# Sums for the means of two LayerNorms as one-column matmuls on TensorE, their sums of squares on GpSimd

## The chip, the cores and the metric

The kernel runs on one core of one Trainium2 chip. The metric is device time in microseconds (us) of one execution. Engines carry the profile's names: PE (TensorE matmuls), PEld (TensorE weight loads), DVE (VectorE), ACT (ScalarE), POOL (GpSimd) and SP (SyncE, which issues the loads).

## The reference

One step of a four-layer backbone on 640 tokens (512 sample tokens and 128 prompt tokens) of 1024 features. Layer i has its own token mixer and then a gated ConvFFN. Every sub-layer first normalises its input and modulates it, and its result is added to the stream, which is normalised again:

```python
# Each sub-layer: h = LN(x)*(1+scale)+shift (adaLN from SiLU(cond)),
# x <- LayerNorm(ALPHA*x + gate*f(h)) (DeepNorm post-norm).
def _layer_norm(x, g=None, b=None):
    xf = x.astype(F32)
    mu = jnp.mean(xf, axis=-1, keepdims=True)
    var = jnp.mean(jnp.square(xf - mu), axis=-1, keepdims=True)
    y = (xf - mu) * lax.rsqrt(var + LN_EPS)
    ...

def _pool_mix(h, w_grp, scale):            # the mixer of layer 2
    ...
    p = (mean - hg.astype(F32)).astype(h.dtype)     # mean over a window of tokens, less h
    y = jnp.einsum('btgc,gcd->btgd', p, w_grp).reshape(B, T, D)
    return y * scale
```

So two LNs stand between any two sub-layers: the post LN of the one that ends and the pre LN of the one that begins, which here is called the inner LN.

## The kernel before, in words

Everything is held feature-major: the stream `x` is 8 ktiles of 128 features (partitions) by 640 tokens. Tokens are worked on in two halves. In most places half 0 is the first 256 tokens and half 1 the last 384; in front of the pooling, which reads neighbouring tokens, half 2 is the first 384 and half 3 the last 256. While one half goes through its two LNs, PE works on the other half or on the next sub-layer.

An LN sums over features, that is over the 8 ktiles and over the 128 partitions. `sums_new` makes two accumulators of a half, `sums_add` is called for each ktile as it is written: ACT squares it (L328 for the first ktile, L332 for the others), POOL adds the ktile to the sum of values (L333), and DVE or POOL adds the square to the sum of squares (`sums_end`, L339), one ktile late. `ln_stats` then sums both over the partitions with one-column float32 matmuls against a column `onesD` (L352: two sums times two or three tiles of 128 tokens, into a `st` bank of PSUM); a float32 matmul leaves two records in the trace. The small row of mean, square of the mean, variance and the power -1/2 follows on DVE, ACT, DVE and POOL (L356 to L360), and PE transposes mean and 1/std back over all partitions into `bc` banks (L372). `centre` subtracts the mean (L383), `ln1` multiplies by 1/std (L395), scales and shifts into `x` (L396), and calls `sums_add` for the inner LN; `ln2` does the inner LN's own multiplication (L404) and modulation (L414), whose result is `h`.

A boundary (layer, 0 or 1) is the pair of LNs behind a sub-layer: (1, 1) lies behind the FFN of layer 1 and in front of the pooling (halves 2 and 3), (2, 0) behind the pooling and in front of the FFN of layer 2 (halves 0 and 1). Around the pooling the program goes through four stages, each named here by a letter:

- A: the down projection of layer 1's FFN for half 3 (`project`, triples of matmuls L175 to L177) covers the LNs of half 2.
- B: the pooling of half 0 (`hw` for three token tiles L1072, then `mix(0)`, L1082 and L1089, whose products `evac` adds to `x` on DVE, L436) covers the LNs of half 3, and the post LN of half 0 follows.
- C: `hw` for the last two token tiles and `mix(1)` cover the inner LN of half 0.
- D: the first up-projections of layer 2's FFN in plain float32 for half 0 (`up_mm32`, L487, 64 matmuls) cover the two LNs of half 1. The triples L175 to L177 begin again behind them.

Order: each engine runs its instructions in the program's order, and where generators of two pieces of work are stepped against each other (`LN_A`, `LN_P`, `LN_B` say at which matmul which step of an LN is issued) the order comes from that and from the framework's own scheduling pass; the final order of each engine is fixed before the run. PSUM pools: `mm` 4 banks (products), `bc` 3, `st` 1. A name such as `mm_15657` in an order is one use of a buffer of pool `mm`.

Of the kernel before, what the change touches and what calls it, by code (L numbers as in the profile page):

```python
# [12 lines left out]
AF = mybir.ActivationFunctionType  # L13
# [4 lines left out]
NK = 8  # L18
TS = 512
TP = 128  # L20
T = TS + TP
# [12 lines left out]
# half 0 runs ahead of half 1, and 2 of 3 (in front of the pooling, which reads neighbours)  # L34
HALVES = ((0, 256), (256, 640), (0, 384), (384, 640))
HW = 384
# (start, stop, group) with group 0 = sample, 1 = prompt
SEGS = (((0, 256, 0),), ((256, 512, 0), (512, 640, 1)), ((0, 384, 0),), ((384, 512, 0), (512, 640, 1)))
# ktiles of the FFN between its down-projections
FFN_CHUNKS = ((0, 7), (7, 14), (14, 22))  # L40
SKEW = {None: 7, 2: 6, 3: 6, 1: 6, 0: 6}
# units of a projection's weights that half B finds from half A
KEEP = {None: 4, (0, 0): 3, (1, 1): 5, (3, 1): 5, (1, 0): 3, (3, 0): 5}
# layer 0's modulation, blocks of 512 features, in plain float32
MOD32 = (2, 0)
# SKEW ktiles of the FFN run half A ahead of half B, 2 SKEW units of weights: the last SPLIT of them in split parts
# (SPLIT_AHEAD units ahead of their use), of which half B finds the last KEPT; h is split SPLIT_H units from the end
SPLIT = {None: 6, 3: 11, 2: 4, 1: 7}
SPLIT_POOL = {None: False, 0: 1}
SPLIT_AHEAD = {None: 2, 0: 0}  # L50
SPLIT_H = {None: 12, 2: 11, 1: 14, 3: 5, 0: 14}
KEPT = 2
# steps of the next layer's modulation behind each product of an FFN
BG = {None: 1, 0: 0.95}
# heads of half A in split parts; units of weights ahead of them
A_SPLIT = 4
A_AHEAD = 1
# items of the attention between the scores and the transposes
LAG = 3
# tiles of tokens of half A per block of 512 features of v; units of weights ahead  # L60
VPRE = ((0, 1), (0, 1), (0,), ())
V_AHEAD = 5
# columns (tokens) that the window sums of a tile of 128 tokens reach; which band matrix of a group that is
BAND_RANGE = ((0, 136), (120, 264), (248, 392), (376, 512), (512, 640))
BAND_KIND = (0, 1, 1, 2, 3)
# tiles of the LN; ktiles that are centred ahead (of the two LNs of a half, and of the last)
# [3 lines left out]
# where the steps of an LN are issued (20: sums, broadcasts, 8 ktiles, and again for the next sub-layer's LN):  # L70
# LN_A half A's, in products (8 each) of half B; LN_B half B's (position, steps), in matmuls of half A of the next
# sub-layer; LN_P the same in the pooling
LN_A = {None: (8, 16, 16, 16, 16, 24, 24, 24, 32, 32, 40, 48, 48, 48, 48, 48, 56, 56, 56, 56), (0, 1): (4, 15, 20, 20, 26, 30, 30, 30, 33, 39, 45, 49, 49, 52, 53, 54, 61, 61, 62, 62), (2, 1): (6, 11, 16, 17, 21, 26, 26, 27, 33, 34, 48, 52, 57, 63, 63, 63, 63, 72, 76, 81), (0, 0): (0, 15, 15, 19, 22, 24, 26, 32, 37, 37, 48, 48, 58, 58, 59, 59, 60, 61, 70, 80), (1, 0): (5, 15, 17, 17, 17, 19, 21, 29, 29, 29, 44, 47, 51, 53, 53, 53, 58, 62, 73, 78), (1, 1): (10, 15, 15, 20, 20, 26, 30, 30, 33, 33, 47, 48, 60, 61, 61, 61, 61, 61, 61, 64), (3, 0): (9, 14, 17, 17, 20, 22, 22, 23, 26, 30, 43, 49, 49, 53, 53, 57, 57, 57, 60, 60), (3, 1): (8, 23, 23, 24, 24, 26, 30, 30, 30, 40, 41, 45, 55, 58, 60, 61, 67, 68, 68, 68)}
LN_B = {None: ((8, 1), (16, 9), (56, 1), (64, 9)), (0, 0): ((0, 1), (12, 9), (51, 1), (65, 9)), (2, 0): ((7, 1), (8, 9), (42, 1), (63, 9)), (1, 0): ((12, 1), (16, 9), (52, 1), (53, 9)), (0, 1): ((2, 1), (15, 9), (58, 1), (63, 9)), (2, 1): ((10, 9), (15, 1), (48, 1), (60, 9)), (3, 0): ((8, 1), (23, 9), (58, 9), (65, 1))}
LN_P = ((4, 1), (16, 1), (22, 4), (23, 3), (24, 1), (38, 2), (44, 2), (45, 1), (51, 1), (52, 3), (54, 1))

# columns of the packed per-partition vectors
# [33 lines left out]
class Kern:  # L111
# [45 lines left out]
    def unit(self, src, shape, e=None):  # L157
        """A piece of weights, split exactly into two float32r parts."""
        nc = self.nc
        r = self.raw(shape)  # L160
        self.load(r, src)
        hl = self.hlp.tile([128, 2] + list(shape[1:]), F32R, tag="hl", name=self.nm("hl"))
        nc.scalar.copy(hl[:, 0], r)  # L163
        (e or nc.vector).tensor_sub(hl[:, 1], r, hl[:, 0])  # L164
        return hl

    def split(self, dst, src, e=None):
        """dst [:, 0] + [:, 1] = src exactly."""
        self.nc.scalar.copy(dst[:, 0], src)  # L169
        (e or self.nc.vector).tensor_sub(dst[:, 1], src, dst[:, 0])  # L170

    def mm3(self, out, lhs, rhs, start, stop):
        """out += lhs^T rhs with (hi, lo) pairs of operands."""
# [8 lines left out]
    def table(self, f, x):  # L182
        """Has the tables of an activation function loaded ahead of its use, once x is there."""
        self.nc.scalar.activation(self.small("tab", [128, 1]), x.bitcast(F32), f)

    def consts(self):
# [27 lines left out]
        # modulation [part, chunk, ktile, group]  # L214
        self.mod = [cp.tile([128, 6, NK, 2], F32, name=f"mod{i}") for i in range(DEPTH)]

    def cond_rows(self):
        """silu(cond) along the free dimension, on every partition."""
# [10 lines left out]
    def mod_post(self, L, ft, n, ps, lo=None):  # L229
        """Feature tiles ft .. ft + n (of one chunk) of the modulation of layer L, from its sums [128, n, 2]."""  # L230
# [12 lines left out]
    def mod_mv(self, fb):  # L243
        """512 features of layer 0's modulation: w_mod streams through the tensor engine. Yields after each unit."""
        nc = self.nc
        ps = self.st([4, 512])
        for i in range(4):
            if fb in MOD32:
                # while the loads set the pace: plain float32, nothing to split
# [23 lines left out]
    def mod_dve(self, L, f0, f1):  # L273
        """Feature tiles f0 .. f1 as dot products on the vector engine. Yields after each product."""
# [15 lines left out]
    def bg(self, n):  # L290
        """n steps (on average) of the background work."""
# [18 lines left out]
    def sums_new(self, half):  # L310
        """Sums of z and z^2 over the ktiles, per partition, of a half."""
        w = HALVES[half][1] - HALVES[half][0]
        S = types.SimpleNamespace(first=None, last=None, pool=True, nt=w // 128, n=0)
        if w <= 256:
# [6 lines left out]
    def sums_add(self, S, z, t=None, scale=None, bias=None, pool=True):  # L321
        """S1 += z, S2 += z^2 on a ktile of a half, z = scale t + bias if t is given; the last square waits
        for sums_end."""
        nc = self.nc
        src, kw = (z, {}) if t is None else (t, dict(scale=scale, bias=bias))
        n, S.n = S.n, S.n + 1
        if n == 0:
# [5 lines left out]
        nc.gpsimd.tensor_add(S.s[0], z, S.s[0] if n > 1 else S.first)  # L333
        self.sums_end(S)
        S.last = sq

# [5 lines left out]
    def ln_stats(self, S, half, eps, together):  # L342
        """Mean and 1/std of the tokens of a half, broadcast over partitions, in PSUM. Yields once between the
        sums and the broadcasts, then the two."""
# [4 lines left out]
        st = self.st([128, 2, 3])  # L349
        for q in range(2):  # L350
            for t in range(S.nt):
# [4 lines left out]
        v.tensor_copy(cv[:, 0, n], st[:, 0, n])  # L356
        nc.scalar.activation(w[:, n], st[:, 0, n], AF.Square)
# [18 lines left out]
    def centre(self, MU, half, ahead):  # L376
        """The ktiles of x of a half less their mean, some ahead of their use."""
# [10 lines left out]
    def ln1(self, t, R, L, which, half, k, S=None):  # L388
        """x <- LN(z) g + b on a ktile of a half."""
# [10 lines left out]
    def ln2(self, t, R, L, ch, half, k, box):  # L400
        """h = LN(x)(1 + scale) + shift on a ktile of a half."""
# [18 lines left out]
    def late_steps(self, box):  # L420
        """(hi, lo) of half A of h."""
# [8 lines left out]
    def evac(self, ps, L, ch, m, half, gate=None):  # L430
        """z += gate' * product, in place in x."""
# [8 lines left out]
    def project(self, gs, units, L, ch, after, fill=None, halves=(0, 1)):  # L440
        """z += gate' W^T g; half A runs ahead so that its LN hides behind half B.

        gs: list of (hi, lo) tiles; units(m) -> weights as a function of the ktile."""
# [38 lines left out]
    def up_mm32(self, h32, w):  # L482
        """Half A of a product in plain float32."""
# [45 lines left out]
    def ffn_pre(self, L, box):  # L529
        """Half A of the first ktiles, while half B of h is not there yet: in plain float32, and the last of  # L530
        them in split parts, whose weights half B then uses first."""
# [28 lines left out]
    def ffn(self, L, box, side, after):  # L560
# [7 lines left out]
        def skew():  # L568
            """Half B of the first ktiles."""
# [63 lines left out]
    def boundary(self, L, which, box, pre=None):  # L633
        """after-callback: post LN of sub-layer (L, which) and the h of the next sub-layer."""
# [765 lines left out]
```

## Time and profile before

| | |
|---|---|
| median of 3 runs | 2803.09 us (2801.15 to 2807.25) |
| span of the profiled execution | 2805.7 us |
| PE busy | 2749.6 us (98%) |
| DVE busy | 1973.0 us (70%) |
| ACT busy | 1240.0 us (44%) |
| POOL busy | 407.5 us (15%) |
| mean granted TensorE clock | 0.987 of 2.4 GHz |

The profiled execution lies 0.1% above the median; its span, from the first to the last instruction, is the time of it that the profile gives. Busy time counts the engine's records; several records of PE overlap, so what a matmul costs PE is read from the distance of starts, not from the length of a record. A granted clock of 1.0 is 2.4 GHz and of 0.5 is 1.2 GHz.

### The profile page before, as it was taken

What the parts mean: (1) busy time and instruction counts of PE and PEld (TensorE: products, weight loads), DVE (VectorE), ACT (ScalarE), POOL (GpSimd) and SP (SyncE); (2) the same over time, 40 slices, a digit from 0 to 9 for tenths busy, and PEclk for the clock granted to TensorE, in tenths of its full rate; (3) what the DMA queues carried; (4) which work ended last, traced back from release to release, by engine and by line L of the source; (5) the groups of instructions that cost most, each with busy time, mean ns of one, the idle gap of its engine ahead of it and who ended that gap; (6) DMA issues with size and microseconds to landing.
All of it is one profiled execution on the core that took longest, in us unless ns stands there. A gap on an engine that the chain in (4) does not pass through costs nothing.

```text
span 2805.7 us, 46039 instructions
## 1 busy us (share of the span) xinstructions
PE 2749.6 (98%) x17826; PEld 2636.0 (94%) x17826; DVE 1973.0 (70%) x4263; ACT 1240.0 (44%) x2286; POOL 407.5 (15%) x417
## 2 busy tenths in 40 slices
PE   7999999999999999999999999999999999999998
PEld 4799999999989999999978999999799999999998
DVE  6879977857697887777587878775756558534344
ACT  5656232336496752323367423234532248423233
POOL 1250000024303300000442000005100042000003
PEclk9999999999999999999989999999999999999999
DMA  7735644432402445455104554542422224322221
GB/s 241 259 109 163 198 154 149 156 121 80 134 22 83 136 153 158 149 157 153 56 35 150 151 165 151 158 136 80 161 65 91 68 62 152 97 82 68 83 75 54
DMA packets 99932, 344.70 MB, mean 123 GB/s; under 512 B 11392, under 2 KB 14080, under 8 KB 99584
## 3 DMA queue, kind: packets, MB, share of 16 engines
q1 hardware_dynamic: 99712, 341.74, 38.7%
q8 instruction: 141, 2.31, 0.3%
q14 instruction: 79, 0.65, 0.1%
HBM read 336.19 MB, written 2.88 MB: 121 GB/s over the span
## 4 chain that ended last, share of the span: by engine, by line
PE 88%; DVE 5%; issue 2%; ACT 2%; DMA 2%; POOL 1%; POOLq 0%; ACTq 0%; SPq 0%; DVEq 0%
PE mm L175 26%; PE mm L176 26%; PE mm L177 26%; PE mm L487 2%; PE st L352 1%; PE mm L1157 1%; DVE hl L164 1%; DVE tmp L339 1%; DMA raw<-in_wmod 1%; PE mm L1247 1%; PE bc L372 1%; DVE lnt L383 1%; DVE act L170 0%; PE mm L1072 0%; DMA raw<-in_wup 0%
## 5 line engine op out<-in xcount | busy, mean ns | idle before, releaser
L177 PE MATMUL mm<-act,hl 128*128 128x384 f32 (+2 forms) x4928 | 1528.5, 310 | 3.2 <-DVE hl L164 3.2
L175 PE MATMUL mm<-act,hl 128*128 128x384 f32 (+2 forms) x4928 | 1531.5, 311 | 0.0
L176 PE MATMUL mm<-act,hl 128*128 128x384 f32 (+2 forms) x4928 | 1528.6, 310 | 1.2 <-POOL act L418 1.2
L177 PEld LDWEIGHTS mm<-act,hl 128*128 128x128 f32 x4928 | 935.1, 190 | 5.0 <-DVE hl L164 4.4
L176 PEld LDWEIGHTS mm<-act,hl 128*128 128x128 f32 x4928 | 935.9, 190 | 3.7 <-POOL act L418 1.8
L175 PEld LDWEIGHTS mm<-act,hl 128*128 128x128 f32 x4928 | 935.2, 190 | 3.2 <-ACT hl L163 0.6
L163 ACT CAST hl<-raw 128x1024 fp32r<-128x1024 f32 (+1 forms) x433 | 444.1, 1030 | 625.9 <-PE mm L177 560.1
L164 DVE TENSOR_TENSOR hl<-raw,hl 128x1024 fp32r<-128x1024 f32 (+1 forms) x428 | 526.0, 1231 | 67.4 <-ACT hl L163 65.1
L283 DVE SCALAR_TENSOR_TENSOR bc<-raw,cbc 128x512 f32<-128x512 f32 x608 | 406.2, 719 | 130.3 <-DMA raw<-in_wmod 130.0
L436 DVE SCALAR_TENSOR_TENSOR x<-mm,mod,x 128x256 f32<-128x256 f32 (+2 forms) x408 | 166.0, 434 | 200.4 <-PE mm L177 199.8
L514 DVE SCALAR_TENSOR_TENSOR tmp<-ap,vecs,tmp 128x512 f32<-128x512 f32 x352 | 170.5, 547 | 147.6 <-ACT tmp L512 147.4
L333 POOL TENSOR_TENSOR tmp<-x,tmp 128x256 f32<-128x256 f32 (+1 forms) x180 | 178.0, 993 | 153.2 <-DVE x L436 109.0
L527 POOL MEMSET ap<- 128x1 f32 x24 | 2.1, 99 | 1188.4 <-DVE tmp L514 735.3
L502 ACT COPY ap<-mm 128x256 f32<-128x256 f32 x88 | 33.0, 375 | 265.2 <-PE mm L177 265.2
L333 POOL TENSOR_TENSOR tmp<-x 128x256 f32<-128x256 f32 (+1 forms) x30 | 30.7, 1024 | 733.3 <-DVE x L436 694.5
L383 DVE TENSOR_TENSOR lnt<-x,bc 128x256 f32<-128x256 f32 (+1 forms) x240 | 109.6, 479 | 14.9 <-PE bc L372 14.4
L332 ACT ACTIVATE lnt<-x 128x256 f32<-128x256 f32 (+1 forms) x112 | 51.2, 467 | 133.3 <-DVE x L436 130.9
L516 ACT ACTIVATE tmp<-tmp 128x640 f32<-128x640 f32 x88 | 65.2, 740 | 100.4 <-DVE tmp L514 100.4
L169 ACT CAST act<-tmp 128x640 fp32r<-128x640 f32 x117 | 84.9, 726 | 52.1 <-DVE tmp L519 31.8
L512 ACT ACTIVATE tmp<-ap,vecs 128x512 f32<-128x512 f32 (+1 forms) x176 | 106.4, 658 | 0.0
L339 DVE TENSOR_TENSOR tmp<-tmp,lnt 128x384 f32<-128x384 f32 (+1 forms) x126 | 93.7, 745 | 14.1 <-ACT lnt L332 12.6
L487 PE MATMUL mm<-h,raw 128*128 128x256 f32 x416 | 101.2, 399 | 1.8 <-DVE lnt L404 1.8
(209 smaller groups left out, 2684.1 us busy)
## 6 DMA issues: line engine op xcount, KB each, us to landing
raw<-in_wup SPq DMA_DIRECT2D x216, 512.0 KB, 3.5
raw<-in_wmod SPq DMA_DIRECT2D x184, 512.0 KB, 3.5
raw<-in_wdn SPq DMA_DIRECT2D x64, 448.0 KB, 3.4
raw<-in_wdn SPq DMA_DIRECT2D x46, 512.0 KB, 3.6
raw<-in_wgv SPq DMA_DIRECT2D x24, 512.0 KB, 4.1
raw<-in_wgo SPq DMA_DIRECT2D x19, 512.0 KB, 3.9
raw<-in_wqk SPq DMA_DIRECT2D x18, 512.0 KB, 3.5
raw<-in_wgu SPq DMA_DIRECT2D x16, 512.0 KB, 3.5
```

Source lines behind the costliest of these rows:

```text
L163: nc.scalar.copy(hl[:, 0], r)
L164: (e or nc.vector).tensor_sub(hl[:, 1], r, hl[:, 0])
L175: t.matmul(out, lhs[0], rhs[0], start=start, stop=False)
L176: t.matmul(out, lhs[0], rhs[1], start=False, stop=False)
L177: t.matmul(out, lhs[1], rhs[0], start=False, stop=stop)
L283: nc.vector.scalar_tensor_tensor(out=self.bc(), in0=r[:, sl], scalar=1.0, in1=self.cbc[:, g, sl], op0=ALU.mult, op1=ALU.mult, accum_out=ac ...
L333: nc.gpsimd.tensor_add(S.s[0], z, S.s[0] if n > 1 else S.first)
L339: (self.nc.gpsimd if S.pool else self.nc.vector).tensor_add(S.s[1], S.s[1], S.last)
L383: self.nc.vector.tensor_sub(t, self.x[:, k, a:b], MU)
L436: nc.vector.scalar_tensor_tensor(out=self.x[:, m, s0:s1], in0=ps[:, s0 - a:s1 - a], scalar=sc, in1=self.x[:, m, s0:s1], op0=ALU.mult, op1= ...
L487: self.nc.tensor.matmul(ps, w[:, k, :], h32[:, k, :], start=k == 0, stop=k == NK - 1)
L514: nc.vector.scalar_tensor_tensor(out=c[:, sl], in0=ap[:, o + i:o + i + n], scalar=cw(i), in1=c[:, sl], op0=ALU.mult, op1=ALU.add)
```

## The change

At the boundaries listed in a new table `PE_MEAN`, which are (1, 1) and (2, 0), the inner LN gets its sums another way. The sum of values is no longer accumulated by POOL: for every ktile of `x`, PE does a one-column float32 matmul for each tile of 128 tokens, accumulating over the ktiles in a bank taken from the pool `mm` (`S.ps`); the matmuls of a ktile are issued one ktile late. The additions of squares go to POOL instead of DVE (`pool = True`, only the last stays on DVE). The sum over partitions of the squares stays one matmul per token tile; the mean is read from `S.ps`. Sums for the post LNs, and all other boundaries, are untouched.

```diff
+PE_MEAN = ((1, 1), (2, 0))
 ...
-    def sums_new(self, half):
+    def sums_new(self, half, pe=False):
         w = HALVES[half][1] - HALVES[half][0]
-        S = types.SimpleNamespace(first=None, last=None, pool=True, nt=w // 128, n=0)
-        if w <= 256:
+        S = types.SimpleNamespace(first=None, last=None, pool=True, nt=w // 128, n=0, ps=None, zs=[])
+        if pe:
+            S.ps = self.mm([128, S.nt])
+            S.s = (None, self.tmp([128, w]))
+        elif w <= 256:
 ...
         n, S.n = S.n, S.n + 1
+        if S.ps is not None:
+            self.sums_pe(S)
+            S.zs.append((n, z))
+            pool = True
 ...
-        nc.gpsimd.tensor_add(S.s[0], z, S.s[0] if n > 1 else S.first)
+        if S.ps is None:
+            nc.gpsimd.tensor_add(S.s[0], z, S.s[0] if n > 1 else S.first)
         self.sums_end(S)
         S.last = sq
+
+    def sums_pe(self, S):
+        for n, z in S.zs:
+            for t in range(S.nt):
+                self.nc.tensor.matmul(S.ps[:, t:t + 1], z[:, 128 * t:128 * t + 128], self.onesD, start=n == 0 and t == 0,
+                                      stop=n == NK - 1, skip_group_check=True)
+        S.zs = []
 ...
         st = self.st([128, 2, 3])
+        mean = st[:, 0]
+        if S.ps is not None:
+            self.sums_pe(S)
+            mean = S.ps
         for q in range(2):
+            if q == 0 and S.ps is not None:
+                continue
 ...
-        v.tensor_copy(cv[:, 0, n], st[:, 0, n])
-        nc.scalar.activation(w[:, n], st[:, 0, n], AF.Square)
+        v.tensor_copy(cv[:, 0, n], mean[:, n])
+        nc.scalar.activation(w[:, n], mean[:, n], AF.Square)
 ...
-            S = self.sums_new(half)
+            S = self.sums_new(half, (L, which) in PE_MEAN)
```

Two places of PE's order show what this moves. Line numbers of the changed kernel are higher: its L352 is the new sum of values, L377 what was L352, L397 what was L372, L1097 what was L1072, L512 what was L487.

The first is the beginning of stage C on PE, where the post LN of half 0 ends (`bc_15302`) and the last token tiles of `hw` begin. Before:

```order
L352 MATMUL st_15290<-onesD,tmp_15193 128x1 x4
L372 MATMUL bc_15302<-identr,lnv_15295 128x128 x2
L1072 MATMUL mm_15467<-raw_15060,act_14733 128x256
L372 MATMUL bc_15302<-identr,lnv_15295 128x128 x2
L1072 MATMUL mm_15473<-raw_15060,act_14733 128x256
L1072 MATMUL mm_15467<-raw_15060,act_14733 128x256
```

The same place after the change:

```order
L377 MATMUL st_15312<-onesD,tmp_15215 128x1 x2
L397 MATMUL bc_15324<-identr,lnv_15317 128x128 x4
L352 MATMUL mm_15352<-onesD,x 128x1 x2
L1097 MATMUL mm_15497<-raw_15074,act_14733 128x256 x2
L1097 MATMUL mm_15497<-raw_15074,act_14734 128x256
L352 MATMUL mm_15352<-onesD,x 128x1 x2
L1097 MATMUL mm_15503<-raw_15074,act_14733 128x256 x2
```

The sum of the first normalised ktile of half 0 (`mm_15352<-onesD,x`) now stands in front of every matmul of `hw`; the other seven stand between those of `hw` and `mix(1)`.

The second place is the beginning of stage D on PE, where `mix(1)` has ended and the up-projections of the FFN for half 0 begin. Before (the first rows are up-projections, `h_15329` being half 0's `h`; `st_15603` the sums of half 1's post LN, `bc_15619` and `bc_15623` its mean and 1/std):

```order
L487 MATMUL mm_15594<-h_15329,raw_15592 128x256 x3
L487 MATMUL mm_15695<-h_15329,raw_15693 128x256 x3
L352 MATMUL st_15603<-onesD,tmp_15491 128x1 x3
L487 MATMUL mm_15712<-h_15329,raw_15710 128x256 x6
L352 MATMUL st_15603<-onesD,tmp_15492 128x1 x3
L487 MATMUL mm_15712<-h_15329,raw_15710 128x256 x2
L372 MATMUL bc_15619<-identr,lnv_15610 128x128 x3
L372 MATMUL bc_15623<-identr,lnv_15610 128x128 x3
L487 MATMUL mm_15728<-h_15329,raw_15726 128x256 x8
```

The same place after the change (`h_15351` is `h`, `st_15633` the sums of the post LN, `mm_15657` the new sums of values of the inner LN):

```order
L512 MATMUL mm_15624<-h_15351,raw_15622 128x256 x8
L377 MATMUL st_15633<-onesD,tmp_15521 128x1 x3
L377 MATMUL st_15633<-onesD,tmp_15522 128x1 x3
L397 MATMUL bc_15649<-identr,lnv_15640 128x128 x3
L397 MATMUL bc_15653<-identr,lnv_15640 128x128 x3
L352 MATMUL mm_15657<-onesD,x 128x1 x3
L512 MATMUL mm_15739<-h_15351,raw_15737 128x256 x3
L352 MATMUL mm_15657<-onesD,x 128x1 x3
```

Before, 16 up-projections stood in front of the first sums, 22 in front of the second and 24 in front of the transposes. Now 8 stand in front of the sums, none between them and the transposes, and none between the transposes and the sum of the first normalised ktile. Behind that, six more sums of values stand two or three up-projections apart from each other, then 18 up-projections, then the last sum of values with the sum of squares, and the rest.

## Rows read from the trace of the kernel before

**Rows 1.** Stretches: busy PE, PEld, DVE, ACT, POOL (records), clock, DMA share, GB/s.

```profile
1380.00:1520.00 140.00, 129.43 (x720) 113.51 (x720) 112.48 (x253) 89.62 (x187) 60.95 (x67) 0.87 0.21 69
1540.00:2805.70 1265.70, 1252.52 (x8211) 1217.80 (x8209) 782.15 (x1579) 480.44 (x810) 123.02 (x131) 0.99 0.34 105
```

**Rows 2.** PE's waits from 1340 to 1520 us: total, times, longest.

```profile
PE st L352 <- POOL tmp L333: 4.9, 3, 2.2
PE mm L487 <- DVE lnt L404: 1.8, 1, 1.8
PE bc L372 <- POOL lnv L360: 1.7, 2, 1.0
```

**Rows 3.** Short stretches at half clock, columns as in group 1.

```profile
1399.80:1406.20 6.40, 6.40 (x31) 6.32 (x32) 2.78 (x10) 0.59 (x2) 4.87 (x7) 0.50 0.75 266
1499.00:1505.00 6.00, 6.00 (x17) 4.92 (x17) 2.71 (x5) 2.21 (x4) 1.71 (x1) 0.50 0.53 175
1430.70:1444.00 13.30, 10.70 (x34) 8.16 (x35) 11.20 (x33) 6.61 (x18) 4.43 (x7) 0.50 0.00 0
1461.50:1463.50 2.00, 1.93 (x9) 1.52 (x7) 0.72 (x4) 0.00 (x0) 1.68 (x3) 0.50 0.00 0
```

**Rows 4.** PE's timeline: sums at full clock, and at half clock (stage B).

```profile
1379.68 1.40 PE L352 MATMUL st<-onesD,tmp 128*128 128x1 f32 x12
1380.94 0.36 PE L175 MATMUL mm<-act,hl 128*128 128x256 f32 x1
...
1435.78 1.96 PE L352 MATMUL st<-onesD,tmp 128*128 128x1 f32 x8
```

**Rows 5.** PE's timeline in stage A: sums and first transposes, half 2.

```profile
1399.24 1.15 PE L352 MATMUL st<-onesD,tmp 128*128 128x1 f32 x6 [2.18 <-POOL tmp L333]
...
1404.23 0.84 PE L372 MATMUL bc<-identr,lnv 128*128 128x128 f32 x3
```

**Rows 6.** Groups of instructions from 1380 to 1510 us, shapes apart.

```profile
L339 DVE TENSOR_TENSOR tmp<-tmp,lnt 128x384 f32<-128x384 f32 x21 | 16.3, 778 | 0.7 <-ACT lnt L332 0.2
L339 POOL TENSOR_TENSOR tmp<-tmp,lnt 128x256 f32<-128x256 f32 x6 | 5.0, 840 | 0.0
```

**Rows 7.** PE's timeline in stages B and C.

```profile
1440.35 5.84 PE L1072 MATMUL mm<-raw,act 128*128 128x256 f32 x18
...
1453.55 0.44 PE L1082 MATMUL mm<-tmp 1*128 1x384 f32 x1
...
1455.03 0.44 PE L1082 MATMUL mm<-tmp 1*128 1x384 f32 x1
...
1462.79 0.63 PE L372 MATMUL bc<-identr,lnv 128*128 128x128 f32 x2
1465.23 10.14 PE L487 MATMUL mm<-h,raw 128*128 128x256 f32 x32 [1.81 <-DVE lnt L404]
```

**Rows 8.** ACT's timeline: the first normalised ktile of half 0.

```profile
1441.78 0.60 ACT L396 ACTIVATE x<-lnt,vecs 128x256 f32<-128x256 f32 x1 [0.20 <-DVE lnt L395]
```

**Rows 9.** DVE's timeline in stage D: half 1's last square.

```profile
1475.17 0.55 DVE L339 TENSOR_TENSOR tmp<-tmp,lnt 128x384 f32<-128x384 f32 x1
```

**Rows 10.** PE's timeline in stage D, up to the first triple.

```profile
1478.47 0.72 PE L352 MATMUL st<-onesD,tmp 128*128 128x1 f32 x6
...
1481.13 0.54 PE L372 MATMUL bc<-identr,lnv 128*128 128x128 f32 x3 [0.63 <-POOL lnv L360]
1481.50 13.12 PE L487 MATMUL mm<-h,raw 128*128 128x256 f32 x60
1496.85 0.83 PE L352 MATMUL st<-onesD,tmp 128*128 128x1 f32 x6 [2.23 <-POOL tmp L333]
...
1505.54 0.82 PE L372 MATMUL bc<-identr,lnv 128*128 128x128 f32 x6
...
1506.44 0.47 PE L175 MATMUL mm<-act,hl 128*128 128x256 f32 x1
```

**Rows 11.** ACT's timeline, stage D: the first normalised ktile of half 1.

```profile
1482.36 0.71 ACT L396 ACTIVATE x<-lnt,vecs 128x384 f32<-128x384 f32 x1 [0.56 <-DVE lnt L395]
```

## The prediction

> **What bounds the kernel now.** The table of stretches comes first. From 1540 us to the end PE is busy 1252.52 of 1265.70 us [rows 1], so what is lost before that is not won back later: a delay of PE around the pooling goes into the time one for one, and so does a gain. Only from 1380 to 1520 us is there slack: PE is busy 129.43 of 140 us, that is 10.6 us idle, and its granted clock is 0.87 there [rows 1]. The view of waits says what the idle time is: PE's sums wait three times for POOL's additions of values, 4.9 us together, once 1.8 us for DVE's first `lnt` of half 0, twice for POOL's power, 1.7 us [rows 2]; the rest is below a microsecond each. The short stretches say that the clock sits at 0.50 (1.2 GHz) for 6.4 us behind the first long wait, for 6 us behind the last, and for most of stage B's end, 1430.7 to 1444 [rows 3]. So two things can be gained, the waits and the time at half clock, and one must be paid, PE's new matmuls.
>
> **What a new matmul costs.** Twelve records, six one-column matmuls at full clock, take from 1379.68 to 1380.94, which is 0.105 us a record and 0.21 us a matmul [rows 4]. At half clock eight records took 1.96 us, 0.49 us a matmul [rows 4]. There are 24 new ones in A (eight ktiles of three token tiles), 16 in B, 16 in C and 24 in D, 80 in all; 3, 2, 2 and 3 old ones, the sums of values over partitions, go. Net 70 x 0.21 = 14.7 us of PE at full clock. That is what has to be hidden in 10.6 us of idle time or paid back by clock. A sentence of the Trainium skill speaks for less: "TensorE: Matmul & The Clock Gate", section "Back-to-back issue gap", gives for 1 to 64 columns a floor of some 25 ns from one start to the next, by which 140 records would be 3.5 us. The rows have four times that, 105 ns a record, since each record here carries a weight load of its own; the trace decides.
>
> On the other side, DVE loses 24 additions of squares, 0.78 us each when 384 wide [rows 6], and POOL loses the additions of values and takes the squares at 0.84 us (256 wide) [rows 6]. For 384 wide the trace has none on POOL; I take 0.84 to 1.5 times that, 1.26 us, at either end less than ACT's two operations for each ktile, 2 x 0.71 [rows 11], so POOL keeps pace. Both count for nothing by themselves; what counts is which event PE waits for in each stage.
>
> **Stage A.** The sums of half 2 arrive later on PE by eight sets of three matmuls, 8 x 0.63 = 5.0 us, less the three removed, 0.6: 4.4 us. They waited 2.18 us for POOL [rows 5]; PE being later by more than that, the wait goes, and with it, if nothing else stalls, the 6.4 us at half clock behind it [rows 3], in which 3.2 us were lost. Between the sums and the transposes of 1/std PE had 5.0 us of sums and triples at half clock (1399.24 to 1404.23) [rows 5]; at full clock those are about 2.5 us, less than the row of small operations behind the sums, which takes 3.2 us in stage D (below), and three old sums fewer stand between: I set 1.0 us of wait for it. 4.4 - 2.2 - 3.2 + 1.0 = 0.0. Bounds: -1.0 without that wait, +3.2 if the clock falls all the same.
>
> **Stage B.** 16 matmuls less 2, 2.9 us, against waits that mostly stand on the same events: mix's squares (still DVE's) end the stage, and the order puts them behind the last `evac`. I take +0.5; bounds -5.0 (first rival) and +2.9 (nothing hidden).
>
> **Stage C.** Before, `hw` began behind the transposes at 1440.35 without a wait [rows 7]. Now the first sum of values stands ahead of it and needs the first normalised ktile, which ACT had ready at 1441.78 + 0.60 = 1442.4 [rows 8], and which takes the same chain as before (subtract, multiply, scale). PE waits 2.0 us, and `hw`, for which nothing was late, waits with it. From 1440.35 to the end of the last transposes at 1462.79 + 0.63 = 1463.4 were 23.1 us of work [rows 7]; with 14 matmuls more, 2.9 us, `mix(1)` ends at 1442.4 + 23.1 + 2.9 = 1468.4, 5.0 later. The wait of 1.81 us for `lnt` [rows 7] should go: the second pair of transposes now stands eleven matmuls ahead of the end of `mix(1)`; five of these took 1.47 us (1453.55 to 1455.03) [rows 7], so they are done by 1465.2, and the 2.4 us that `lnt` and `h` needed behind them (1462.79 to 1465.23) [rows 7] end before PE comes.
>
> **Stage D.** Half 1's last square was done at 1475.17 + 0.55 = 1475.7 [rows 9], 12.3 us behind the end of those transposes (1463.4). In between DVE did half 0's inner LN, seven squares and the last evacuations, and it does the same now: DVE's relief lies earlier. So the sums may start at 1465.2 + 12.3 = 1477.5. PE has eight up-projections ahead of them, 16 records of the 32 that took 10.14 us [rows 7], 5.1 us, and is there at 1473.5: about 4 us of wait, where before 24 up-projections covered everything. From the second sums to the end of the transposes it was 1478.47 to 1481.13 + 0.54, 3.2 us [rows 10]: now bare, 1480.7. The first normalised ktile came 1482.36 + 0.71 - 1481.67 = 1.4 us behind that [rows 11]: bare too, 1482.1. Left for PE then: 56 up-projections, 112 records at 13.12/60 = 0.219 [rows 10], 24.5 us; 24 sums of values and three of squares, 54 records, 5.7 us; six transposes, 0.8 us [rows 10]. The wait of 2.23 us [rows 10] goes, since seven of the new sums are spread among 16 up-projections, and 18 more cover the squares. At full clock the first triple comes at 1482.1 + 31.0 = 1513.1. Before, 6 us at half clock [rows 3] cost 3.0 us here; behind waits of 4, 3 and 1.4 us in a row I leave half of that, 1.5. First triple at 1514.6 instead of 1506.44 [rows 10]: +8.2. This contains C.
>
> **Sum.** 0.0 + 0.5 + 8.2 = +8.7 us. The profiled span of 2805.7 would be 2814.4; against the median, from which it stands 2.6 us, 2803.1 + 8.7 = 2811.8, say **2812 us**. A difference of 0.2%, 5.6 us, is about what a measurement of this kernel can tell from none.
>
> **Rivals.**
>
> *It gets faster (0.15).* POOL and DVE are relieved, and the new matmuls fill idle time. The price hangs on stage B: if they keep PE busy there, the stretch from 1430.7 to 1444 runs at 2.4 GHz. It holds 10.7 us of work [rows 3], half of it lost to the clock, 5.3 us, and some 2.6 us of waits besides (13.3 - 10.7); against 2.9 for the matmuls B gives -5.0. A at its lower bound gives -1.0. In D the wait of 2.23 and the 3.0 at half clock go against 21 net matmuls, 4.4: -0.8. C gives +2.9 - 1.8 = +1.1. Sum -5.7, 2797.4 us. It decides by whether the normalised ktiles stand ready when PE reaches their sums. Against it: the first ktile comes 2.0 us behind PE in C and 1.4 us in D [rows 8, 11], and in both places nothing else stands in front of its sum.
>
> *It cancels (0.20).* The matmuls cost 14.7 us, and nearly all of the slack is recovered: waits of 4.9 and 1.8 us [rows 2], and 3.2 and 3.0 at half clock in A and D [rows 3]: +1.8, 2805 us. Against it is what the order shows in D: the cover of 24 up-projections is cut to 8. It would hold if DVE's squares of half 1 end well ahead of 1477.5.
>
> *The clock stays low (0.13).* In 1461.5 to 1463.5 the clock stood at 0.50 although PE was busy 1.93 of 2 us [rows 3], on short matmuls. If sums and waits keep it there through C and D, the 31.0 us of D run at 1.2 GHz for some 10 us more of loss, and the sums of C (0.49 instead of 0.21) for another 3. Then +8.7 + 13 - 1.5 = +20.2, 2823 us. The Trainium skill, same page, "What's actually happening", says the same of direction, that the gate follows how busy the array has been; it gives no time here.
>
> **How the numbers follow.** The forecast gets 0.52, from 2807 to 2818, where its terms move between the bounds of A and half a half-clock stretch more or less in D. For 8 in 10 the range has to take in cancelling and part of both outer cases: 2798 to 2821. Faster by over 0.2% takes the first rival's half and a little of others, 0.13; within 0.2% (2797.5 to 2808.7) the rest of it, cancelling and the forecast's lower edge, 0.25; slower 0.62.
>
> **What would show it.** In the changed trace: PE's new sums about 0.6 us for three (A), and no wait for POOL at the sums of half 2; an idle stretch of some 2 us on PE behind the post LN's transposes of half 0, released by ACT, ahead of `hw`; an idle stretch of some 4 us behind the first eight up-projections, released by DVE's squares; two more of 3 and 1.4 us behind it; the first triple some 8 us later against the last triple of A; no change after 1540 but the shift. I am wrong if PE finds half 1's squares ready behind the eight up-projections, or if stage B and the clock give back more than 3 us.

## The result, and the profile after

The changed kernel takes 2835.86 us (median of 4 runs, 2830.85 to 2837.15) against 2804.27 us before (4 runs): ratio 1.0109, 95% interval 1.0095 to 1.0123. It is slower, as forecast, but by 31.6 us between the medians (30.6 by the ratio) where 8.7 were forecast, and outside the range of 2798 to 2821 us. The profiled execution took 2830.85 us, span 2829.1; that of before took 2807.25. The spans differ by 23.4 us, less than the medians, because the first happens to be the fastest of its kernel and the second the slowest. What follows compares these two.

The stretches of the changed kernel (columns as in [rows 1]):

```profile
1406.00:1421.00 15.00, 14.74 (x80) 12.71 (x80) 9.85 (x27) 12.13 (x24) 2.85 (x4) 1.00 0.01 2
1421.00:1450.00 29.00, 24.69 (x95) 21.38 (x96) 15.87 (x47) 12.14 (x30) 9.47 (x15) 0.50 0.00 0
...
1478.20:1483.70 5.50, 0.00 (x0) 0.00 (x0) 5.50 (x10) 3.38 (x10) 2.96 (x3) 0.90 0.29 95
1483.70:1510.00 26.30, 23.67 (x80) 20.27 (x81) 10.65 (x25) 10.23 (x18) 6.86 (x7) 0.50 0.06 20
1510.00:1531.00 21.00, 21.00 (x113) 18.80 (x112) 6.90 (x12) 7.61 (x15) 0.85 (x1) 1.00 0.58 177
```

Two long stretches at 1.2 GHz stand out, 29 and 26.3 us, where before there were four of 6 to 13 us. [rows 3] show three of them in full; of the fourth they show 2 us, but it lasted from 1461 to 1471:

```profile
1461.00:1471.00 10.00, 8.19 (x25) 6.64 (x26) 8.53 (x23) 6.17 (x13) 3.18 (x4) 0.50 0.00 0
```

PE's waits in the changed kernel, in the same part of the program, 1340 to 1560 us:

```profile
PE st L377 <- POOL tmp L344: 5.6, 1, 5.6
PE bc L397 <- POOL lnv L385: 3.5, 5, 1.0
PE mm L352 <- ACT x L421: 3.3, 2, 1.8
```

The three waits for POOL's values [rows 2] have become one of 5.55 us, and two waits for normalised ktiles are new. PE's timeline, stage by stage:

```profile
1382.89 0.73 PE L352 MATMUL mm<-onesD,x 128*128 128x1 f32 x6
...
1401.76 0.54 PE L397 MATMUL bc<-identr,lnv 128*128 128x128 f32 x3 [0.83 <-POOL lnv L385]
...
1418.42 0.95 PE L352 MATMUL mm<-onesD,x 128*128 128x1 f32 x8
...
1419.61 0.85 PE L1114 MATMUL mm<-act,act 128*128 128x136 f32 x6
...
1430.56 1.50 PE L1114 MATMUL mm<-act,act 128*128 128x136 f32 x6
...
1445.76 0.69 PE L397 MATMUL bc<-identr,lnv 128*128 128x128 f32 x2 [0.96 <-POOL lnv L385]
1448.26 1.01 PE L352 MATMUL mm<-onesD,x 128*128 128x1 f32 x4 [1.81 <-ACT x L421]
...
1474.12 4.04 PE L512 MATMUL mm<-h,raw 128*128 128x256 f32 x16
1483.72 2.72 PE L377 MATMUL st<-onesD,tmp 128*128 128x1 f32 x12 [5.55 <-POOL tmp L344]
...
1490.86 1.44 PE L352 MATMUL mm<-onesD,x 128*128 128x1 f32 x6 [1.45 <-ACT x L421]
...
1530.93 0.47 PE L177 MATMUL mm<-act,hl 128*128 128x256 f32 x1
```

Six matmuls of `mix(0)` of one form take 0.85 us at 1419.61 and 1.50 at 1430.56; no wait stands in between. The wait at 1483.72 is put down to POOL's last addition of values for the post LN, but DVE's squares for it end just as late (the last addition at 1483.87 + 0.55). The waits of 1.81 and 1.45 us are the two first ktiles.

From the first sums in stage A (half 2's post LN) to the first triple behind D it was 1379.68 to 1506.44, 126.8 us [rows 4, 10]; now it is 1376.59 to 1530.93, 154.3: 27.6 us longer. The rest of the program behind it is 1 us shorter, and the changed execution came to stage A 3 us earlier. By stages, from marker to marker (first `hw`; end of the post LN's transposes of half 0; end of `mix(1)`; first triple):

| stage | forecast | measured |
|---|---|---|
| A | 0.0 | +1.0 |
| B | +0.5 | +8.0 |
| C | +5.0 | +4.9 |
| D | +3.2 | +13.8 |

### The profile page after: what moved, and what is told of

The parts are those of the page before. It is cut to its first block, busy times and chain, and to the rows that moved or that the text cites. A ratio compares the mean times of both kernels' runs of the same rounds, so it can differ in the third digit from the quotient of the medians.

```text
span 2829.1 us, 46263 instructions
## 1 busy us (share of the span) xinstructions
PE 2768.8 (98%) x17966; PEld 2654.1 (94%) x17966; DVE 1953.2 (69%) x4239; ACT 1239.5 (44%) x2286; POOL 396.2 (14%) x413
## 4 chain that ended last, share of the span: by engine, by line
PE 89%; DVE 5%; issue 2%; ACT 2%; DMA 1%; POOL 1%; POOLq 0%; SPq 0%; ACTq 0%; DVEq 0%
PE mm L177 26%; PE mm L178 26%; PE mm L179 26%; PE mm L512 2%; DVE hl L166 1%; PE mm L1182 1%; PE st L377 1%; PE mm L352 1%; DVE tmp L358 1%; PE mm L1097 1%; PE mm L1272 1%; PE bc L397 1%; DVE lnt L408 1%; PE mm L1114 1%; DMA raw<-in_wmod 0%
## 5 line engine op out<-in xcount | busy, mean ns | idle before, releaser
L344 POOL TENSOR_TENSOR tmp<-x,tmp 128x256 f32<-128x256 f32 (+1 forms) x156 | 153.0, 984 | 155.0 <-DVE x L461 126.4
L358 POOL TENSOR_TENSOR tmp<-tmp,lnt 128x384 f32<-128x384 f32 (+1 forms) x108 | 115.5, 1071 | 26.1 <-ACT lnt L342 24.7
L512 PE MATMUL mm<-h,raw 128*128 128x256 f32 x416 | 102.9, 401 | 0.0
```

Of the source, the lines that this page charges most:

```text
L358: (self.nc.gpsimd if S.pool else self.nc.vector).tensor_add(S.s[1], S.s[1], S.last)
L512: self.nc.tensor.matmul(ps, w[:, k, :], h32[:, k, :], start=k == 0, stop=k == NK - 1)
```

## The experiments

Each profiled execution is read with one account. Over the 240 stretches of one microsecond from 1360 to 1600 us I add up PE's idle time, and PE's busy time multiplied by what the granted clock lacks to 1.00 (lost to clock). The work that PE has more is counted at full clock, 0.21 us a one-column matmul [rows 4]; the wide form of two runs below is 0.64 us for 384 columns (14 records in 4.51 us, shown below) and 0.44 for 256 (two records of 0.219 [rows 10]). "Sum" is the work and the two differences from before, "measured" the stretch from A's first sums to the triple behind D, less 126.8. Times are medians, with the ratio to the runs of before on the same chip. The account reads one execution of each kernel, and that of before is the slowest of its four, so "measured" and the difference of the medians can part by several microseconds.

| kernel | us | ratio, interval | work | idle | lost to clock | sum | measured |
|---|---|---|---|---|---|---|---|
| before | 2804 | | | 10.6 | 16.4 | | |
| changed | 2835.9 | 1.0109 (1.0095 to 1.0123) | 14.7 | 14.5 | 25.0 | +27.2 | +27.6 |
| (1, 1) alone | 2812.7 | 1.0031 (1.0021 to 1.0041) | 7.4 | 9.0 | 19.2 | +8.6 | +9.1 |
| (2, 0) alone | 2832.5 | 1.0097 (1.0080 to 1.0114) | 7.4 | 14.0 | 30.2 | +24.6 | +24.5 |
| sums last | 2822.7 | 1.0061 (1.0042 to 1.0081) | 14.7 | 9.5 | 10.7 | +7.9 | +6.8 |
| constant | 2840.9 | 1.0131 (1.0116 to 1.0146) | 16.8 | 14.6 | 26.5 | +30.9 | +22.9 |
| wide | 2820.3 | 1.0051 (1.0036 to 1.0066) | 17.3 | 13.7 | 8.8 | +12.8 | +13.4 |
| squares on DVE | 2828.3 | 1.0088 (1.0066 to 1.0110) | 14.7 | 11.6 | 25.7 | +25.0 | +24.4 |
| engines swapped | 2813.3 | 1.0034 (1.0022 to 1.0047) | 0 | 17.6 | 12.0 | +2.6 | +3.0 |
| last value on DVE | 2811.7 | 1.0021 (1.0011 to 1.0031) | 0 | 16.2 | 13.9 | +3.1 | +3.3 |
| D alone, last | 2812.9 | 1.0033 (1.0022 to 1.0044) | 4.4 | 10.8 | 21.7 | +9.9 | +8.7 |
| D alone, wide, last | 2803.1 | 0.9998 (0.9989 to 1.0007) | 5.2 | 8.3 | 13.0 | -0.5 | -0.7 |
| wide, last | 2810.3 | 1.0018 (1.0008 to 1.0027) | 17.3 | 4.9 | 8.9 | +4.1 | +3.9 |

**One boundary each.** First only the one in front of the pooling, then only the one behind it.

```diff
-PE_MEAN = ((1, 1), (2, 0))
+PE_MEAN = ((1, 1),)          # and, in the other run, ((2, 0),)
```

> Only boundary (1, 1), in front of the pooling, gets the new sums (stages A and B); from stage C on PE's order is that of the kernel before. Theory (clock): the sums of values that stand among the short matmuls of mix(0) bring TensorE's clock to 1.2 GHz from its beginning on, although PE is busy all the time; A costs 1 us and B 8 us, as in the changed kernel, so about 2804 + 9 = 2813 us, with the granted clock at 0.50 from about 1421 to 1450. Rival (waits): the loss lies in the waits of C and D and in what they do to the clock; this half of the change then costs only its uncovered matmuls, 1 to 3 us, 2805 to 2807 us, and the clock in mix(0) stays at 1.00 up to about 1430 as before.

> Only boundary (2, 0), behind the pooling, gets the new sums (stages C and D); up to the post LN of half 0 PE's order is that of the kernel before. Both theories expect the two uncovered first ktiles (2 and 1.4 us), a wait for half 1's squares behind eight up-projections of some 5 us, and half clock behind it. Theory (each stage pays by itself): C 4.8 and D 13.8 as in the changed kernel, about 2804 + 18.6 = 2823 us. Rival (carried over): D stalls that long because B delivers late and at half clock; with B as before, C and D cost no more than the 8 us forecast, about 2812 us.

The first is slower by 0.31%, 2812.7 us, as the first theory had it. Its stretch behind the first sums in `mix(0)`:

```profile
1424.00:1447.00 23.00, 21.28 (x83) 18.35 (x82) 11.89 (x36) 9.75 (x25) 8.78 (x13) 0.50 0.00 0
```

PE is busy 21.28 of 23 us, and the clock stands at 0.50 from early in `mix(0)` on. Waits do not bring this about, so the first theory holds here. The second kernel:

```profile
1415.70:1426.00 10.30, 9.43 (x60) 8.08 (x60) 9.38 (x22) 8.75 (x21) 8.00 (x11) 0.98 0.01 2
1426.00:1443.00 17.00, 11.64 (x40) 9.06 (x41) 13.93 (x41) 9.08 (x22) 5.68 (x9) 0.51 0.00 0
1456.00:1473.00 17.00, 17.00 (x61) 13.97 (x60) 11.53 (x32) 7.12 (x15) 4.43 (x6) 0.51 0.00 1
1480.00:1511.00 31.00, 28.72 (x89) 24.43 (x90) 10.96 (x22) 12.70 (x23) 6.78 (x7) 0.50 0.11 34
```

With no new sums in it, `mix(0)` keeps 0.98 to its end. At 1456, in `mix(1)`, the clock falls, in a stretch in which PE was busy 17.00 of 17.00 us. That the sums of C did this is not shown: in the kernel before it fell in `mix(1)` too, at 1461, without them, and in the changed kernel, which has the same sums there, it stayed up:

```profile
1452.00:1478.00 26.00, 25.34 (x151) 20.41 (x149) 14.81 (x45) 15.89 (x34) 8.07 (x11) 1.00 0.12 42
```

D stays at half clock for 31 us. The rival, that D only inherits B's delay, falls: this boundary costs 27 to 28 us by itself. That is some 9 us more than the first theory's 18.6, so the theory missed too. The two together would be 36 us against 32 for both at once, so the pieces do not add.

**The sums at another place.** The matmuls of all ktiles are issued when the inner LN's sums end.

```diff
         if S.ps is not None:
-            self.sums_pe(S)
             S.zs.append((n, z))
             pool = True
```

> As the changed kernel, but the sums of values of all eight ktiles are issued together at the end of the inner LN, not one ktile late each; same matmuls, same additions on POOL. In PE's order mix(0) is free of them up to its last product, and in D 16, 22 and 24 up-projections stand again in front of the first sums, the second and the transposes. Theory (clock and cover): mix(0) runs at 1.00 up to about 1430, the wait of 5.55 us in D is gone, and of the 32 us some 10 to 15 are left, for the matmuls themselves: 2814 to 2819 us. Rival (work): the 80 matmuls and the late squares cost what they cost wherever they stand, 2830 us or more.

The median is +18 us, 2822.7, between the theory's 2814 to 2819 and the rival's 2830, and the four runs spread from 2816.6 to 2828.3. The profiled one is the fastest, with a mean granted clock of 0.990 against 0.985 in the two slowest:

```profile
1410.00:1438.00 28.00, 27.55 (x171) 24.04 (x171) 18.28 (x47) 19.56 (x40) 11.27 (x16) 0.99 0.00 1
1438.00:1455.00 17.00, 11.38 (x40) 9.09 (x41) 13.35 (x42) 7.95 (x19) 3.63 (x5) 0.51 0.00 1
1455.00:1514.00 59.00, 57.08 (x336) 50.01 (x335) 34.32 (x85) 35.17 (x74) 18.42 (x20) 1.00 0.31 96
```

`mix(0)` runs at full clock to its end, and D, with 24 up-projections ahead of its transposes again, waits for POOL 0.37 and 0.56 us only and has no half clock. The bank `S.ps` is held here too, so it is the place of the sums in the order, not the bank, that cut D's cover from 24 up-projections to 8. The rival (work) falls, since it is the same work. In A the clock falls here too: behind 42 records of sums in a row (4.94 us from 1395.76), with no wait in front, it is at 0.50 from 1401 to 1410, where before it was for 6.4 us, behind a wait of 2.18 [rows 3, 5].

**The matmuls without their data.** The kernel before with 80 one-column matmuls on a constant; DVE copies the result of each LN once, and it is not used.

```diff
         n, S.n = S.n, S.n + 1
+        if S.ps is not None:
+            for t in range(S.nt):
+                nc.tensor.matmul(S.ps[:, t:t + 1], self.ident, self.onesD, start=n == 0 and t == 0, stop=n == NK - 1,
+                                 skip_group_check=True)
```

> The kernel before, all sums as there, plus the 80 one-column matmuls at the places of the new ones in the program, but on a constant that is always ready, into a bank held as in the changed kernel; their result is not used. In PE's order they stand in sets of 16, 16 and 24 in front of mix(0), behind it and behind the first up-projection of D, no longer one ktile at a time. Theory (clock by interleaving): a set among long matmuls costs 0.21 us each, 24 of them hidden in A at that price too; 80 x 0.21 = 17 us less what falls into idle time: 2812 to 2819 us, with mix(0) at full clock. Rival (waits): matmuls that wait for nothing fill the 10.6 us of idle time, and cost at most 6 us, up to 2810 us. Rival (clock by number): any 16 of them put the clock at 0.50 and it costs as much as the change, 2830 us or more.

Here my theory missed, and the third reading, clock by number, held: +36 us, at least as much as the change itself. PE's timeline in front of and in `mix(0)`:

```profile
1420.35 3.19 PE L1079 MATMUL mm<-raw,act 128*128 128x256 f32 x14
1423.37 3.66 PE L330 MATMUL mm<-onesD,identr 128*128 128x1 f32 x32
1426.96 0.57 PE L1089 MATMUL mm<-tmp 1*128 1x256 f32 x1
1427.47 1.50 PE L1096 MATMUL mm<-act,act 128*128 128x136 f32 x6
```

and its stretch behind that:

```profile
1427.00:1461.00 34.00, 31.41 (x120) 27.51 (x120) 17.94 (x51) 10.76 (x26) 9.65 (x13) 0.50 0.00 0
```

Sixteen one-column matmuls, 32 records without a gap and without anything to wait for, and the clock stands at 0.50 behind them for 34 us. Interleaving is not needed. In the table this kernel's sum and measure differ by 8 us; 5.5 of them are a wait of PE for DVE's split of weights behind D, which the sum counts and the measured stretch does not reach.

**The same sums in another form.** One matmul of 256 or 384 columns per ktile, at nearly the same places, behind the same data.

```diff
-            S.ps = self.mm([128, S.nt])
+            S.ps = self.mm([128, w])
 ...
-            for t in range(S.nt):
-                self.nc.tensor.matmul(S.ps[:, t:t + 1], z[:, 128 * t:128 * t + 128], self.onesD, ...)
+            self.nc.tensor.matmul(S.ps, self.onesD.to_broadcast([128, 128]), z, start=n == 0, stop=n == NK - 1)
 ...
-            mean = S.ps
+            m = self.tmp([128, b - a])
+            nc.scalar.copy(m, S.ps)          # then one-column matmuls of m with a unit column
```

> The changed kernel with its new sums in another form: for each ktile one matmul of a matrix of 1/1024 with the ktile as moving operand, 256 or 384 columns, into the same bank, instead of two or three one-column matmuls; at full clock 0.44 or 0.66 us a ktile against 0.42 or 0.63, at the same places and behind the same data. (At the end ACT copies the sum to SBUF, and two or three one-column matmuls bring the mean into the old form: about 1 us of chain for each of the four LNs.) Theory (the form): one-column matmuls between short matmuls bring the clock down; with columns in its place the clock stays at 1.00 through mix(0), and what is left is the 15 to 17 us of PE work and 4 us of idle time, 2820 to 2825 us. Rival (the work as such, and the waits): the clock falls in mix(0) as in the changed kernel, 2835 us or more.

+16 us, as the theory had it, where the one-column form costs 32. The long waits are the same:

```profile
PE st L376 <- POOL tmp L344: 5.6, 1, 5.6
PE mm L351 <- ACT x L420: 3.3, 2, 1.8
```

The clock is not:

```profile
1423.00:1437.00 14.00, 12.80 (x80) 10.74 (x80) 9.46 (x25) 8.60 (x21) 9.48 (x13) 0.99 0.00 1
1437.00:1447.00 10.00, 6.91 (x20) 5.05 (x21) 7.34 (x24) 7.31 (x18) 2.10 (x4) 0.51 0.00 0
...
1478.00:1491.00 13.00, 10.36 (x29) 7.50 (x30) 10.09 (x24) 6.77 (x12) 4.23 (x5) 0.50 0.00 0
1491.00:1519.00 28.00, 28.00 (x133) 23.67 (x132) 6.77 (x12) 11.18 (x22) 3.50 (x4) 1.00 0.46 153
```

`mix(0)`, which begins at 1422.85, keeps 0.99 with the sums among it, and behind the same wait of 5.55 us the clock is back after 13 us instead of 26. With 2.6 us more of work, PE loses 16 us less to the clock (8.8 against 25.0). The other executions agree: the mean granted clock is 0.990 or 0.991 in all four of this kernel, and 0.982 to 0.986 in the four of the changed one. So the form of the matmul, not the wait and not the work, makes the difference. The wide form has more columns in a matmul and one matmul with its weight load where the other has two or three; which of these counts was not tested.

**The two parts of the change.** Values on TensorE with the squares left on DVE, and the squares on POOL with the values on DVE, nothing on TensorE.

```diff
-            pool = True                      # first run: squares stay on DVE
...
-        nc.gpsimd.tensor_add(S.s[0], ...)    # second run, at the two boundaries, no bank and no matmul
+        (nc.vector if S.dv else nc.gpsimd).tensor_add(S.s[0], ...)
```

> One part of the change alone: the new sums of values on TensorE, but the squares stay on DVE. Theory (TensorE's sums are the whole cost): as the changed kernel within 4 us, 2831 to 2840 us. Rival (POOL's slower squares come late and pull the stages apart): 10 us or more of the 32 go, 2825 us or less.

> The other part alone, with nothing on TensorE: at the two boundaries POOL adds the squares and DVE the values, so the two engines only change places; no new matmul and no bank held. Theory (TensorE's sums are the whole cost): as before within 5 us, 2799 to 2809 us. Rival (POOL's squares): 2814 us or more.

The first costs 24 us, between what the theory and the rival gave. The difference of some 7 us from the change is not clear of noise, since the two intervals overlap; most of the cost, in any case, comes with the sums on TensorE. The second costs 9 us, between the theory's 5 and the rival's 10. It moves the values to DVE as well, so it does not price the squares' move alone. Its longest waits in the stretch:

```profile
PE mm L1093 <- ACT act L435: 4.3, 3, 1.8
PE bc L393 <- POOL lnv L381: 3.5, 4, 2.1
PE st L373 <- DVE tmp L340: 3.0, 3, 1.8
```

PE now waits for DVE's values more than for POOL's; longer still are the waits of `hw` for ACT's modulation, 4.3 us, which were 0.2 us before. Only 3 us are found in the pooling of the profiled execution (table). Its span is 4.8 us longer than that of before, not 9, and 1.0 of them arise ahead of stage A, where PE's order is the same.

**The kernel before, its waits for POOL attacked directly.**

```diff
-        nc.gpsimd.tensor_add(S.s[0], z, S.s[0] if n > 1 else S.first)
+        (nc.vector if S.dv and n == NK - 1 else nc.gpsimd).tensor_add(S.s[0], z, S.s[0] if n > 1 else S.first)
```

> The kernel before with the smallest move that could take the waits of TensorE for POOL: at the two boundaries DVE adds the last of the eight ktiles to the sum of values, POOL the other six as before. Theory (work, idle time and clock add up): the waits of 2.18 and 2.23 us shorten by about 1 us each or go, and with them one or both of the half-clock stretches of 6 us behind them (3 us lost each): 2794 to 2802 us. Rival (the clock falls at some other place of these stages, for the short matmuls): within 3 us of before, 2801 to 2807 us.

Both expectations missed: 7.5 us slower. PE's waits for POOL's values shrink from 4.9 us in three to 1.1 in one, waits for DVE take their place, and the waits for POOL's power grow from 1.7 us [rows 2] to 4.3:

```profile
PE bc L372 <- POOL lnv L360: 4.3, 6, 1.3
PE st L352 <- DVE tmp L333: 3.1, 2, 1.6
...
PE st L352 <- DVE tmp L339: 1.3, 1, 1.3
PE st L352 <- POOL tmp L333: 1.1, 1, 1.1
```

The pooling is 3.3 us longer in this execution; 4.0 of the 7.6 us between the spans arise ahead of stage A, where PE's order is that of before.

**Stage D alone, in both forms.** The new sums only for half 1 behind the pooling, issued last.

```diff
-            S = self.sums_new(half, (L, which) in PE_MEAN)
+            S = self.sums_new(half, (L, which, half) == (2, 0, 1))
```

> The new sums in stage D alone (boundary (2, 0), half 1), all issued at the end of the inner LN; A, B and C are the kernel before, instruction for instruction on PE. From the first up-projection to the first triple behind stage D the kernel before takes 41.2 us, the one with all sums last 37.8 us, with 21 matmuls more. Theory (in D the sums fill the wait for POOL and keep the clock up): 3 us faster than before, 2799 to 2802 us. Rival (stage D of that profile was a lucky course of the clock): the matmuls' own 4.4 us show, 2805 to 2810 us.

> As the run with D's sums last, but one 384-column matmul for each ktile instead of three one-column ones (and ACT's copy and three more one-column matmuls at the end). Theory (the form sets the clock): the clock stays at 1.00 to the end of D at least as often; equal or up to 3 us faster than that run, 2797 to 2802 us. Rival (the longer chain at the end decides): 1 to 3 us slower than that run.

> The changed kernel with both edits: wide sums, and all of them at the end of each inner LN. Theory (PE work, idle time and clock add up, form and cover are separate): the wide form took 15 us off the 32, the place another 5 to 10 through the wait of 5.6 us in D; 2810 to 2816 us. Rival (both edits take away the same loss, the clock): 2817 to 2822 us, as each of them alone.

The one-column form is 0.33% slower, so the good stage D of the run with all sums last was a favourable course of the clock: its rival's 2805 to 2810 was even too low. The wide form does not differ from before and is 9.7 us below the one-column form, where the theory allowed at most 3. In front of the sums PE's order is the same in both. One-column, PE's timeline and the stretch:

```profile
1490.55 4.26 PE L351 MATMUL mm<-onesD,x 128*128 128x1 f32 x30
1494.67 3.76 PE L511 MATMUL mm<-h,raw 128*128 128x256 f32 x8
```

```profile
1493.00:1507.00 14.00, 14.00 (x48) 12.20 (x49) 0.51 (x1) 3.12 (x6) 1.55 (x2) 0.52 0.24 75
```

Wide:

```profile
1487.42 4.68 PE L350 MATMUL mm<-x,onesD 128*128 128x384 f32 x14
1491.93 1.03 PE L510 MATMUL mm<-h,raw 128*128 128x256 f32 x4
```

```profile
1469.00:1504.00 35.00, 34.37 (x169) 28.82 (x168) 21.42 (x44) 21.58 (x43) 8.90 (x9) 0.99 0.47 152
```

Four and a half microseconds of sums either way. Behind the one-column ones eight records of the up-projection take 3.76 us, 0.47 each, and the clock is down for 14 us in which PE is busy 14.00; behind the wide ones four take 1.03, 0.26 each, and it never falls. From the first up-projection to the first triple D takes 46.8 us in the one profile and 40.5 in the other; the medians of the two kernels, which differ in nothing else that is large, are 9.7 us apart (2812.85 against 2803.11).

The loss does not come in every execution. The profiled one-column execution is the slowest of seven (2818.62 us, mean clock 0.986); the fastest took 2805.07 at 0.993. And in the profile with all sums last the same 30 records stand behind the same 36 of the up-projection, and the clock stays at 1.00 (its stretch from 1455 above):

```profile
1497.80 3.40 PE L351 MATMUL mm<-onesD,x 128*128 128x1 f32 x30
1501.07 1.97 PE L511 MATMUL mm<-h,raw 128*128 128x256 f32 x8
```

All sums wide and last come to 0.18% above before, 2810.25 us, the lower edge of what the theory gave and less than either edit alone. The form took 16 us off the 32 and the place 13; together they took 26, so the two nearly add. No version is faster than the kernel before beyond its interval.

## Why the prediction was wrong

**What held.** The direction; the price of a matmul (0.59 us from the first set of three to the next triple in A, against 0.63); stage A within 1.0 us (a wait of 0.83 for POOL's power against 1.0, the wait of 2.18 and its half clock gone); stage C to 0.1 us, with 1.81 us for the first ktile against 2.0; in D the late sums (9.6 us behind the end of `mix(1)` against 9.1) and the second uncovered ktile, 1.45 against 1.4. The wait in front of those sums was 5.55 us against about 4, because the prediction priced the eight up-projections at 5.1 us from a row of 10.14 us whose first six ran at half clock, and they took 4.04; that the sum of the two came out is partly luck. The floor of some 25 ns a start in the Trainium skill ("TensorE: Matmul & The Clock Gate", section "Back-to-back issue gap") is not what sets the pace here, as argued ahead: the records stand 0.1 us apart.

**The step that failed** is the clock, in three places. First, stage B: "I take +0.5", between a gain from the clock and the bare work. It cost 8.0 us, outside its bounds of -5.0 and +2.9, since the one-column sums brought the clock to 0.50 from 1421 on; no bound allowed for that. Second, in D: "I leave half of that, 1.5". The chain behind the wait and the 31.0 us of work ran at half clock until 1510: from 1483.72 to 1490.86 it was 7.1 us instead of 4.6 (3.2 and 1.4; the 3.2 begin at the second of two sets of sums, and both stood behind the wait), and from there to the first triple 40.1 instead of 32.5. Third, the first rival made a gain of the same matmuls in B and shifted the range's lower side. In the account, the forecast of +8.7 was 14.7 of work and -6.0 of idle time and clock together; measured were +3.9 of idle time and +8.6 of clock.

**Why I had it so.** I read the half-clock stretches of before [rows 3] as the trail of waits, and took it that a PE without gaps keeps its clock. Two of the four follow waits of over 2 us; in front of the one at 1430 stood waits of 0.37 and 0.51 us only. The fourth, at 1461.5 with PE busy 1.93 of 2 us on short matmuls, I gave to a rival with a chance of 0.13, and did not see that it lasted 10 us. That rival named the right mechanism for D. It was mis-sized, too: C did not lose what it gave it (the clock was at 1.00 from 1452 to 1478), and it had nothing for B, where the clock fell first. The runs on form (wide against one-column, 16 us in all and 9.7 us in D alone) and on matmuls without data (+36 us) decide it: the waits alone do not make the loss. The Trainium skill, "TensorE: Matmul & The Clock Gate", section "What's actually happening", says that the gate is set by how busy the array has been lately. If busy is read off PE's records, the trace of the one-column form in D alone disagrees: busy 14.00 of 14.00 us, and the clock at 0.52. The measurement decides.

**Relief of POOL and DVE** bought nothing that PE could use: swapping the engines or moving one addition replaced waits for POOL's values by waits for DVE, for ACT's modulation and for POOL's power.

**Open.** Why the kernels without new matmuls are 7.5 and 9 us slower when 3 us show in the pooling of one execution of each; what it is in the one-column form that lets the clock fall; and how often a given order loses the clock, since the executions of one kernel differ by up to 13.9 us (squares on DVE).

## What to carry to other kernels

Price a new matmul twice: by its own time, and by what it does to the granted clock of the stretch around it, above all among work that is short already. If a sum over partitions must go to TensorE, compare a constant matrix (here of 1/1024) with the data as moving operand: here it cost the same time, 0.64 against 0.63 us for 384 tokens, and kept the clock in `mix(0)` and in D alone. And look where a new instruction stands that waits for another engine: in an in-order queue it uncovers everything behind it, and issuing it late restored D's cover.

## What was not expected of the hardware

Sixteen one-column float32 matmuls in a row (32 records, 3.66 us, PE without a gap) were followed by 34 us at 1.2 GHz, while 14 records of 384 columns in 4.68 us left the clock at 0.99. It is not certain each time: 30 one-column records in 3.40 us among the up-projections kept 1.00 in one kernel's profile, and in another's the same 30 were followed by 14 us at 0.52. A clock that had fallen stayed down through all of `mix(0)` although PE was busy for most of it, and came back during longer matmuls: in the changed kernel at 1452 during `hw` and at 1510 during the up-projections, both 256 columns wide.
